# Reordering one feed-forward stage of a hybrid decoder layer: which forms are made first, and which column groups are mixed plain

## The chip, the cores and the metric

One NeuronCore of one Trainium2 chip runs the kernel. The metric is the device time of one execution in microseconds (us). The kernel before took 1992.39 us as the median of 3 runs (1990.27 to 1993.79).

## The reference, cut to what matters

One decoder layer on 256 tokens of 2048 channels, all in float32:

```
h = layer_norm(ALPHA * x + 0.5 * swiglu(x, ffn1...))
h = layer_norm(ALPHA * h + mixer(h))
h = layer_norm(ALPHA * h + 0.5 * swiglu(h, ffn2...))
swiglu(x) = (silu(x @ w_gate) * (x @ w_up)) @ w_down     # 2048 -> 5632 -> 2048
```

The change lies in the products `x @ w_gate` and `x @ w_up` of the two feed-forward networks (FFN1 and FFN2). Gate and up columns are interleaved in advance, so that a block of 512 output columns holds 256 gate and 256 matching up columns. There are 22 such blocks.

## The kernel before, in words

**Numbers.** Every float32 operand is cut in two: a high part, which ScalarE rounds off with a copy (`split`, line 149), and a low part, which VectorE gets by a subtraction (line 150). A product is three matmuls (`triple`, lines 202 to 204): high x with high w, high x with low w, low x with high w. So the first matmul of a unit needs ScalarE alone, and the second needs VectorE too. A weight unit is two k tiles of 128 rows by 512 columns; it is loaded by SyncE into `raw` or `sraw`, then split into a pair of the ring (`wring`).

**Run-ahead.** `unit` (line 188) queues the load, the split and the products of a unit. `look(3, 4)` lets three units be loaded and four be split ahead of the products. The ring has 10 pairs in the first stage of an FFN and 6 afterwards (`set_ring`, called in `second` at its unit 6), so a split waits until the products that used the pair are done. `tick` counts units whose products have been issued, and `later(n, f)` calls f after n ticks. The code's order isn't quite the order in an engine's queue: the program is put in order when it is built, and the trace shows the result.

**The gate and up stage of an FFN** (`ffn`, line 763). Blocks 0 and 1 are plain: `project` runs 8 units each, every unit giving 12 matmuls (2 k tiles, 2 halves of the tokens, 3 matmuls). When a half of a block is done, ScalarE takes silu of the gate (`sg`, line 773) and VectorE multiplies (`hb`, line 777); VectorE turns the block (`blocks`, line 664) and GpSimd writes it to DRAM.

Blocks 2 to 21 go in ten groups of two, p = 1 to 10 (`Hybrid.group`). A group computes a 2 x 2 block product (two halves of the tokens by two column blocks) over two sets of k tiles with seven products in place of eight. Products 1 to 7 use fixed linear forms of x, made once (`Seven`: the forms of k tiles 0 to 7, tiles `xs`), and sums of weight blocks, made on the way: products 5, 6 and 4 add two weight tiles on VectorE (line 390), and for product 7 a GpSimd DMA adds a weight block into an `sraw` tile in place (line 392). Each of these has two steps of 2 k tiles, 6 matmuls a step. The other k tiles are plain units: `p` for the first column block, `q` for the second.

A group is **wide** or not. A wide group takes k tiles 8 and 9 into the seven products as well: a third step of one tile (3 matmuls, weights in `eraw`, forms `xe` and `xm` made by `Extra.make`), and then only three `p` and three `q` units. A group that is not wide has four `p` and four `q` units. In matmuls: 14 x 6 + 7 x 3 + 6 x 12 = 177 in a wide group and 14 x 6 + 8 x 12 = 180 in the other. Before the change p = 1, 2, 4, 5, 7, 8 and 10 are wide, and 3, 6 and 9 are not.

The order inside a group is a string: `15p6pp72q4q3q` for a wide one, `15p6pp7p2q4q3qq` for the other, and `1p5p6p7p3q2q4qq` for the mixer's groups (`small`). After product 1 the FFN groups seed bank Y with minus X (`begin`, line 364, ScalarE), so that result (0, 0) comes out of the bank without a subtraction. The mixer's groups keep a copy of X (`n1`) and subtract it at the end (`gus` in `sum_done`, line 789, for an FFN).

**The forms.** In `first_hook`, ahead of unit 5 of block 0, six steps are planned: `sums` (the four differences), the pair for products 5 and 6, the pair for 7 and 3, the forms of 2 and 4 as they are, minus for product 1, and at last `extra.make`, at ticks 1, 3, 5, 7, 9 and 11. Block 1 ends at tick 11. `extra.make` is four subtractions of 128 x 128 (`fe`, line 312), a split of 128 x 512 (`xe`) and a negated split of 128 x 128 (`xm`, lines 323 and 324). It also holds the last use of the third raw tile of x.

**What else the groups carry.** During group 10, `get_h` and `split_h` fetch and split two tiles of h for the down product, at ticks 13 and 16 (four splits of 128 x 512). The down product (`Sliced`) follows, then LayerNorm; the mixer lies between the two FFNs.

**Buffers.** All large tiles share 41 slots (`act_tile`), PSUM banks are five `mm` and three `tr`.

Of the kernel before, what the change touches and what calls it, by code (L numbers as in the profile page):

```python
# [59 lines left out]
def layer_kernel(ctx: ExitStack, tc: tile.TileContext, a: dict, out: bass.AP):  # L60
# [6 lines left out]
    small = ctx.enter_context(tc.tile_pool(name="small", bufs=1))  # L67
# [17 lines left out]
    def mm_bank(name="mm"):  # L85
        return psum.tile([P, 512], F32, tag="mm", name=nm(name), bufs=5)
# [16 lines left out]
    def later(n, fn):  # L103
        uid[0] += 1
        heapq.heappush(todo, (step[0] + n, uid[0], fn))
# [42 lines left out]
    def split(hi, lo, src):  # L148
        S.copy(hi, src)  # L149
        V.tensor_tensor(out=lo, in0=src, in1=hi.bitcast(F32), op=ALU.subtract)  # L150
# [37 lines left out]
    def unit(load, prep, now, later_on=None):  # L188
        if load is not None:
            load()  # L190
        loaded.append((prep, now, later_on))
        advance(*ahead)

    def next_pair():
        assert len(ring) > len(prepared) + lag[0], (len(ring), len(prepared), lag[0])
        catch_up(len(ring) - 1)
        pair = ring.pop(0)
        ring.append(pair)
        return pair
# [127 lines left out]
    class Hybrid:  # L327
# [11 lines left out]
                        self.raws[n] = self.raws[n] + [t[:, i, :]]  # L339
            self.snaps = [act_tile([P, 2, 512], F32, "snap") for _ in range(2)]  # L340

        def group(self, w0, w1, done, wide=False):
            banks = {}
            small = self.small
            n2, n3, q5, n1 = [t[:, i, :] for t in self.snaps for i in range(2)]
            R = self.raws
            blocks = {"11": (w0, 0), "12": (w1, 0), "21": (w0, 2), "22": (w1, 2)}

            plan = {1: ("11", "11", None, "X"), 5: ("12", "11", ("11", "12"), "Z"), 6: ("22", "11", ("11", "22"), "X"),
                    7: (None, "12", ("12", "22"), "X"), 2: ("21", "21", None, "Y"), 4: (None, "11", ("11", "21"), "W"),  # L350
                    3: (None, "22", None, "Z")}
            after = {1: lambda: S.copy(n1, banks["X"]), 6: lambda: S.copy(n2, banks["X"]),
                     7: lambda: S.copy(n3, banks["X"]), 5: lambda: S.copy(q5, banks["Z"]),
                     2: lambda: done(0, 0, banks["Y"], n1, ALU.subtract),
                     4: lambda: done(0, 1, banks["W"], n3, ALU.subtract)}
            stops = {1, 5, 6, 7, 2, 4}

            def bank(n):
                first = n not in banks
                if first:  # L360
                    banks[n] = mm_bank()
                return banks[n], first

            def begin():
                S.mul(bank("Y")[0], banks["X"], -1.0)  # L365
            if not small:
                after[1] = begin
                after[2] = lambda: done(0, 0, banks["Y"], None, None)

            end_s = 2 if wide else 1  # L370

            def source(name, s):
                w, j0 = blocks[name]
                if s < 2:
                    return w[j0 + s]
                i = j0 // 2
                return w[4][:, i * 512:(i + 1) * 512]

            def seventh(p, s):
                load_block, src, add, b = plan[p]  # L380
                st = {}
                tiles = G if s < 2 else 1

                def load():
                    nc.sync.dma_start(R[load_block][s], source(load_block, s))

                def prep():
                    t = R[src][s]
                    if add is not None and (small or p != 7):
                        V.tensor_tensor(out=t, in0=t, in1=R[add[1]][s], op=ALU.add)  # L390
                    if not small and p == 6:
                        nc.gpsimd.dma_start(R["12"][s], source("22", s), accum_op=ALU.add)  # L392
                    pair = [v[:, :tiles * 512] for v in next_pair()]
                    split(*pair, t)
                    st["pair"] = [v.rearrange("p (g n) -> p g n", g=tiles) for v in pair]

                def now():
                    o, first = bank(b)
                    wh, wl = st["pair"]
                    for g in range(tiles):  # L400
                        if s < 2:
                            xh, xl = (v[:, 2 * s + g, :] for v in self.seven.at_[p])
                        else:
                            xh, xl = self.extra.at_[p]
                        triple(o, xh, xl, wh[:, g, :], wl[:, g, :], first and g == 0,
                               s == end_s and g == tiles - 1 and p in stops, b in "XZ" or not small)
                    if s == end_s and p in after:
                        after[p]()
                unit(load if load_block else None, prep, now)

            def plain(n, j, last=False):
                w = (w0, w1)[n]
                names = (("Y", "W"), ("Z", "X"))[n]
                st = {}

                def load():
                    st["raw"] = wpool.tile([P, 1024], F32, tag="raw", name=nm("raw"), bufs=4)
                    nc.sync.dma_start(st["raw"], w[j])

                def prep():  # L420
                    pair = next_pair()
                    split(*pair, st["raw"])
                    st["pair"] = [v.rearrange("p (g n) -> p g n", g=G) for v in pair]

                def now():
                    wh, wl = st["pair"]
                    for b in range(2):
                        o, first = bank(names[b])
                        for g in range(G):
                            k = 2 * j + g  # L430
                            triple(o, self.x.at(0, k, b), self.x.at(1, k, b), wh[:, g, :], wl[:, g, :],
                                   first and g == 0, last and g == 1, n == 1 or not small)
                    if last:
                        done(1, 0, banks["Z"], n2, ALU.add)
                        done(1, 1, banks["X"], q5, ALU.add)
                unit(load, prep, now)

            end = self.k_tiles // G - 1
            if small:
                order = "1p5p6p7p3q2q4qq"  # L440
            elif wide:
                order = "15p6pp72q4q3q"
            else:
                order = "15p6pp7p2q4q3qq"
            turn = {n: iter(range(5 if wide else 4, end + 1)) for n in range(2)}
            for i, c in enumerate(order):
                if c in "pq":
                    plain("pq".index(c), next(turn["pq".index(c)]), i == len(order) - 1)
                else:
                    for s in range(end_s + 1):  # L450
                        seventh(int(c), s)
# [311 lines left out]
    def ffn(n, x, wgu, wdn, residual, g, bt, each, first=None, between=None, nxt=None, cols=None):  # L763
# [20 lines left out]
        def sum_done(c, b, bank, snap, op):  # L784
            if snap is None:
                gu_done(c, b, bank)
                return
            t = tmp_tile([P, 512], "gus")
            V.tensor_tensor(out=t, in0=bank, in1=snap, op=op)  # L789
            half(c, b, t[:, 256:512], t[:, 0:256])  # L790
# [17 lines left out]
        seven = Seven(x.raws)  # L808
        extra = Extra(x, 2)
# [7 lines left out]
        def first_hook(j):  # L817
            if first is not None:
                first(j)
            if j == 5:  # L820
                for i, f in enumerate(seven.steps + [extra.make]):
                    later(2 * i + 1, f)
        project(wgu[0], x, KD, 512, lambda b, bank: gu_done(0, b, bank), hook=first_hook,
                between=between)
        project(wgu[1], x, KD, 512, lambda b, bank: gu_done(1, b, bank), hook=second)
# [2 lines left out]
        for p in range(1, KF // 4):  # L828
            if p == KF // 4 - 1:
                for i, q in enumerate((3, 4, 0)):  # L830
                    later(3 + 3 * i, lambda q=q: get_h(q))
                later(13, lambda: split_h(3))
                later(16, lambda: split_h(4))
            hy.group(wgu[2 * p], wgu[2 * p + 1],
                     lambda n, b, bank, snap, op, p=p: sum_done(2 * p + n, b, bank, snap, op), p % 3 != 0)
        ln = LayerNorm(0.5, residual, g, bt, each, nxt, cols, ((24, 26, 48, 50), (94, 97, 100, 103)))
        if n == 1:
            later(70, setup)
# [3 lines left out]
        order = (1, 5, 6, 7, 2, 4, 3)  # L842
# [4 lines left out]
        for p in range(2):  # L847
# [30 lines left out]
            else:  # L878
                call(len(units) - 8, widen)
            down.run(wdn[2 * p], wdn[2 * p + 1], units, forms,  # L880
                     lambda m, b, bank, sign, p=p: ln.fold(2 * p + m, b, bank, sign),
                     lambda m, b, bank, p=p: ln.evac(2 * p + m, b, bank), calls, 8 * p)
# [500 lines left out]
```

## Time and profile before

| | us |
|---|---|
| median of 3 runs | 1992.39 (1990.27 to 1993.79) |
| the profiled execution's own time | 1992.18 |
| its span in the profile | 1990.4 |
| FFN1: first product of the groups to the end of group 10 | 53.23 to 462.96 |
| FFN2: the same | 1337.24 to 1748.05 |

The span runs from the first instruction to the last; 1.8 us of the execution's time lie around it. In the profile's rows, a start is in us from the span's start, PE is TensorE, DVE is VectorE, ACT is ScalarE, POOL is GpSimd and SP is SyncE. A row of the timeline has the start, the duration, the engine and line, the operation, the tiles, the shapes and the count, and in brackets the idle time before it with what ended it.

### The profile page before, as it was taken

What the parts mean: (1) busy time and instruction counts of PE and PEld (TensorE: products, weight loads), DVE (VectorE), ACT (ScalarE), POOL (GpSimd) and SP (SyncE); (2) the same over time, 40 slices, a digit from 0 to 9 for tenths busy, and PEclk for the clock granted to TensorE, in tenths of its full rate; (3) what the DMA queues carried; (4) which work ended last, traced back from release to release, by engine and by line L of the source; (5) the groups of instructions that cost most, each with busy time, mean ns of one, the idle gap of its engine ahead of it and who ended that gap; (6) DMA issues with size and microseconds to landing.
All of it is one profiled execution on the core that took longest, in us unless ns stands there. A gap on an engine that the chain in (4) does not pass through costs nothing.

```text
span 1990.4 us, 25588 instructions
## 1 busy us (share of the span) xinstructions
PE 1965.1 (99%) x8790; PEld 1620.4 (81%) x8790; DVE 1767.2 (89%) x2153; ACT 1263.4 (63%) x1645; POOL 297.8 (15%) x517
## 2 busy tenths in 40 slices
PE   9999999999999999999999999999999999999997
PEld 7788888888888887888888888777888888888886
DVE  6999999999898889999977686779999999998886
ACT  5676766766656566666667864556666676666552
POOL 0121112112100011002223130011112211121000
PEclk9999999999999999999999999999999999999999
DMA  8888888878767666677767677658888878696763
GB/s 303 276 236 266 265 277 228 251 218 301 259 218 269 203 229 238 221 243 256 229 205 250 221 232 266 222 212 263 256 262 275 242 231 280 183 332 246 245 216 124
DMA packets 145458, 485.16 MB, mean 244 GB/s; under 512 B 20736, under 2 KB 20784, under 8 KB 145328
## 3 DMA queue, kind: packets, MB, share of 16 engines
q1 hardware_dynamic: 113328, 389.60, 57.0%
q0 software_dynamic: 32000, 93.93, 18.0%
q8 instruction: 69, 1.13, 0.2%
q14 instruction: 61, 0.50, 0.1%
HBM read 454.61 MB, written 28.84 MB: 243 GB/s over the span
## 4 chain that ended last, share of the span: by engine, by line
PE 86%; DVE 8%; issue 2%; DMA 2%; ACT 1%; SPq 0%; DVEq 0%; POOL 0%; ACTq 0%; POOLq 0%
PE mm L203 28%; PE mm L204 27%; PE mm L202 27%; DVE wring L150 4%; DVE sraw L390 2%; PE tr L202 1%; PE tr L203 1%; PE tr L204 1%; DMA sraw<-in_wgm_dram 1%; DVE blocks L664 0%; DVE hb L777 0%; ACT wring L149 0%; PE tr L629 0%; DVE gus L789 0%; DMA turn<-blocks 0%
## 5 line engine op out<-in xcount | busy, mean ns | idle before, releaser
L149 ACT CAST wring<-raw 128x1024 fp32r<-128x1024 f32 (+2 forms) x471 | 486.4, 1038 | 345.4 <-PE mm L204 236.6
L150 DVE TENSOR_TENSOR wring<-raw,wring 128x1024 fp32r<-128x1024 f32 (+2 forms) x471 | 562.1, 1202 | 108.0 <-ACT wring L149 101.1
L149 ACT CAST wring<-sraw 128x1024 fp32r<-128x1024 f32 x436 | 454.4, 1052 | 204.6 <-PE mm L204 68.8
L150 DVE TENSOR_TENSOR wring<-sraw,wring 128x1024 fp32r<-128x1024 f32 x436 | 524.0, 1218 | 20.8 <-ACT wring L149 17.5
L204 PE MATMUL mm<-wring,h 128*128 128x512 f32 (+2 forms) x1254 | 483.2, 386 | 0.9 <-DVE h L150 0.9
L203 PE MATMUL mm<-wring,h 128*128 128x512 f32 (+2 forms) x1254 | 482.5, 385 | 0.3 <-DVE wring L150 0.3
L202 PE MATMUL mm<-wring,h 128*128 128x512 f32 (+2 forms) x1254 | 482.3, 385 | 0.3 <-ACT mm L365 0.2
L203 PE MATMUL mm<-wring,xs 128*128 128x512 f32 x776 | 304.9, 393 | 4.8 <-DVE wring L150 4.7
L202 PE MATMUL mm<-wring,xs 128*128 128x512 f32 x776 | 303.6, 391 | 3.5 <-ACT wring L149 3.4
L204 PE MATMUL mm<-wring,xs 128*128 128x512 f32 x776 | 303.0, 390 | 0.0
L204 PEld LDWEIGHTS mm<-wring,h 128*128 128x128 f32 x1254 | 235.6, 188 | 48.6 <-DVE h L150 2.6
L202 PEld LDWEIGHTS mm<-wring,h 128*128 128x128 f32 x1254 | 235.6, 188 | 47.6 <-ACT h L149 1.1
L203 PEld LDWEIGHTS mm<-wring,h 128*128 128x128 f32 x1254 | 235.7, 188 | 46.7 <-DVE wring L150 0.6
L390 DVE TENSOR_TENSOR sraw<-sraw,sraw 128x1024 f32<-128x1024 f32 x168 | 203.2, 1218 | 2.2 <-DMA sraw<-in_wdq_dram 0.9
L203 PEld LDWEIGHTS mm<-wring,xs 128*128 128x128 f32 x776 | 146.0, 188 | 41.4 <-DVE wring L150 11.7
L202 PEld LDWEIGHTS mm<-wring,xs 128*128 128x128 f32 x776 | 146.0, 188 | 36.4 <-ACT wring L149 5.9
L204 PEld LDWEIGHTS mm<-wring,xs 128*128 128x128 f32 x776 | 146.2, 188 | 29.7
L203 PE MATMUL mm<-wring,x 128*128 128x512 f32 x342 | 133.5, 390 | 0.8 <-DVE wring L150 0.8
L202 PE MATMUL mm<-wring,x 128*128 128x512 f32 x342 | 132.3, 390 | 0.8 <-ACT wring L149 0.8
L204 PE MATMUL mm<-wring,x 128*128 128x512 f32 x342 | 133.1, 390 | 0.0
L666 POOL DMA_DIRECT2D hT<-blocks x176 | 97.0, 562 | 168.5 <-DVE blocks L664 115.1
L392 POOL DMA_DIRECT2D sraw<-in_gu_dram x40 | 35.7, 899 | 524.3 <-DVE sraw L390 515.8
(297 smaller groups left out, 2252.8 us busy)
## 6 DMA issues: line engine op xcount, KB each, us to landing
raw<-in_gu_dram SPq DMA_DIRECT2D x163, 512.0 KB, 4.8
sraw<-in_gu_dram SPq DMA_DIRECT2D x160, 512.0 KB, 5.3
raw<-in_dn_dram SPq DMA_DIRECT2D x140, 512.0 KB, 4.6
sraw<-in_gu_dram POOLq DMA_DIRECT2D x40, 512.0 KB, 6.0
sraw<-in_dn_dram SPq DMA_DIRECT2D x36, 512.0 KB, 6.0
hraw<-hT POOLq DMA_DIRECT2D x68, 256.0 KB, 5.1
raw<-in_w_out_dram SPq DMA_DIRECT2D x32, 512.0 KB, 4.0
eraw<-in_gu_dram SPq DMA_DIRECT2D x56, 256.0 KB, 6.1
```

The lines of the kernel that those rows point to most:

```text
L149: S.copy(hi, src)
L150: V.tensor_tensor(out=lo, in0=src, in1=hi.bitcast(F32), op=ALU.subtract)
L202: PE.matmul(o, xh, wh, start=first, stop=False, skip_group_check=again)
L203: PE.matmul(o, xh, wl, start=False, stop=False, skip_group_check=again)
L204: PE.matmul(o, xl, wh, start=False, stop=last, skip_group_check=again)
L390: V.tensor_tensor(out=t, in0=t, in1=R[add[1]][s], op=ALU.add)
L392: nc.gpsimd.dma_start(R["12"][s], source("22", s), accum_op=ALU.add)
L666: nc.gpsimd.dma_start(to.rearrange("(g r) (i f) -> i r g f", g=4, i=4)[i], t[32 * i:32 * (i + 1), :].rearrange("r (g f) -> r g f", g=4))
```

## The change

It does four things, in both FFNs:

1. `extra.make` comes first, at tick 1, and the steps of `Seven` follow at ticks 2, 4, 6, 8 and 10.
2. Group 1 is no longer wide. The groups that aren't wide are p = 1, 4 and 7; wide are 2, 3, 5, 6, 8, 9 and 10. Their numbers stay 3 and 7.
3. Group 1 has the order `1p5p6p7p2q4q3qq`.
4. Group 1 doesn't seed bank Y: it keeps a copy of X and subtracts it at the end. The other FFN groups seed as before (`seeded`), and the mixer's groups stay as they were.

```diff
-        def group(self, w0, w1, done, wide=False):
+        def group(self, w0, w1, done, wide=False, seeded=False):
...
-            if not small:
+            if seeded:
                 after[1] = begin
                 after[2] = lambda: done(0, 0, banks["Y"], None, None)
...
             elif wide:
                 order = "15p6pp72q4q3q"
+            elif seeded:
+                order = "15p6pp7p2q4q3qq"
             else:
-                order = "15p6pp7p2q4q3qq"
+                order = "1p5p6p7p2q4q3qq"
...
             if j == 5:
-                for i, f in enumerate(seven.steps + [extra.make]):
-                    later(2 * i + 1, f)
+                for i, f in enumerate([extra.make] + seven.steps):
+                    later(2 * i + 1 - (i > 0), f)
...
             hy.group(wgu[2 * p], wgu[2 * p + 1],
-                     lambda n, b, bank, snap, op, p=p: sum_done(2 * p + n, b, bank, snap, op), p % 3 != 0)
+                     lambda n, b, bank, snap, op, p=p: sum_done(2 * p + n, b, bank, snap, op),
+                     p % 3 != 1 or p == 10, p > 1)
```

Two more lines pass `seeded` in place of `not small` to the matmuls' group check.

More of the change, by code (lines that the diff above doesn't have):

```diff
@@ L405, in now @@
                         triple(o, xh, xl, wh[:, g, :], wl[:, g, :], first and g == 0,
-                               s == end_s and g == tiles - 1 and p in stops, b in "XZ" or not small)
+                               s == end_s and g == tiles - 1 and p in stops, b in "XZ" or seeded)
                     if s == end_s and p in after:
@@ L431, in now @@
                             triple(o, self.x.at(0, k, b), self.x.at(1, k, b), wh[:, g, :], wl[:, g, :],
-                                   first and g == 0, last and g == 1, n == 1 or not small)
+                                   first and g == 0, last and g == 1, n == 1 or seeded)
                     if last:
```

## The prediction

> **What bounds the kernel now.** First the page: busy shares and the chain of waits. Then TensorE's idle time by stretches, and the queues around the idle places.
>
> ```profile
> PE 1965.1 (99%) x8790; PEld 1620.4 (81%) x8790; DVE 1767.2 (89%) x2153; ACT 1263.4 (63%) x1645; POOL 297.8 (15%) x517
> PE 86%; DVE 8%; issue 2%; DMA 2%; ACT 1%; SPq 0%; DVEq 0%; POOL 0%; ACTq 0%; POOLq 0%
> ```
>
> TensorE is the bound nearly everywhere, so the change can gain only where TensorE stops. VectorE, at 89%, is the next bound, and holds 8% of the chain. The busy time by stretches, cut at FFN1's groups 1, 2, 3, 4 and 10 and at FFN2's group 1:
>
> ```profile
> 53.23:97.62 44.39, 42.01 (x178) 33.02 (x178) 43.95 (x47) 30.12 (x37) 8.60 (x13) 1.00 0.87 268
> 97.62:138.22 40.60, 40.41 (x179) 33.15 (x177) 40.10 (x46) 27.55 (x35) 6.41 (x11) 1.00 0.83 250
> 138.22:179.30 41.08, 41.08 (x181) 33.70 (x180) 39.25 (x42) 26.31 (x32) 7.71 (x12) 1.00 0.89 258
> 179.30:219.42 40.12, 40.12 (x178) 33.23 (x177) 38.07 (x43) 27.00 (x35) 7.30 (x12) 1.00 0.84 258
> ...
> 422.84:462.96 40.12, 40.12 (x178) 33.23 (x177) 40.12 (x51) 30.17 (x42) 6.08 (x11) 1.00 0.52 157
> ...
> 1337.24:1382.67 45.43, 43.30 (x177) 34.24 (x178) 44.11 (x47) 29.99 (x37) 8.51 (x13) 0.96 0.91 294
> ```
>
> The first number is the length, the fourth busy time is VectorE's. Group 4 shows the floor: 177 matmuls in 40.12 us, 0.2267 each, so a group of 180 needs 40.80. A wide group behind another wide one takes 40.60, the group behind that 41.08: 0.48 and 0.28 over the floor. Rows 2 to 4 repeat up to 422.84. Group 1 is 4.27 over its floor in FFN1 and 5.31 in FFN2, and TensorE stops ahead of it:
>
> ```profile
> 51.38 0.39 PE L204 MATMUL mm<-wring,x 128*128 128x512 f32 x1
> 53.23 0.49 PE L202 MATMUL mm<-wring,xs 128*128 128x512 f32 x1 [1.47 <-ACT wring L149]
> 54.86 0.50 PE L203 MATMUL mm<-wring,xs 128*128 128x512 f32 x1 [1.14 <-DVE wring L150]
> ...
> 1335.44 0.39 PE L204 MATMUL mm<-wring,h 128*128 128x512 f32 x1
> 1337.24 0.49 PE L202 MATMUL mm<-wring,xs 128*128 128x512 f32 x1 [1.41 <-ACT wring L149]
> 1338.93 0.50 PE L203 MATMUL mm<-wring,xs 128*128 128x512 f32 x1 [1.20 <-DVE wring L150]
> ```
>
> From start to start that is 1.85 and 1.80, so 1.62 and 1.57 lost. Lost at the groups' beginning in all: 5.89 in FFN1, 6.88 in FFN2. It isn't that VectorE had no time before:
>
> ```profile
> 39.80:49.50 9.70, 9.70 (x44) 8.04 (x43) 0.00 (x1) 0.38 (x1) 0.00 (x0) 1.00 0.96 351
> ```
>
> Its busy time there is 0.00. What stands in its queue and ScalarE's:
>
> ```profile
> 39.29 0.49 DVE L312 TENSOR_TENSOR fe<-xraw 128x128 f32<-128x128 f32 x2
> 49.50 0.42 DVE L777 TENSOR_TENSOR hb<-mm,sg 128x256 f32<-128x256 f32 x1 [9.72 <-ACT sg L773]
> 49.84 0.61 DVE L312 TENSOR_TENSOR fe<-xraw,fe 128x128 f32<-128x128 f32 x2
> 51.13 0.69 DVE L150 TENSOR_TENSOR xe<-fe,xe 128x512 fp32r<-128x512 f32 x1 [0.69 <-ACT xe L149]
> 51.74 0.28 DVE L324 SCALAR_TENSOR_TENSOR xm<-xraw,xm 128x128 fp32r<-128x128 f32 x1
> ...
> 52.99 0.71 DVE L664 STREAM_TRANSPOSE blocks<-hb 128x512 f32<-128x512 f32 x1
> 53.63 2.32 DVE L150 TENSOR_TENSOR wring<-sraw,wring 128x1024 fp32r<-128x1024 f32 x2
> ```
> ```profile
> 49.08 0.38 ACT L773 ACTIVATE sg<-mm 128x256 f32<-128x256 f32 x1 [11.47 <-PE mm L204]
> 50.48 0.62 ACT L149 CAST xe<-fe 128x512 fp32r<-128x512 f32 x1 [1.01 <-DVE fe L312]
> ...
> 51.86 0.38 ACT L773 ACTIVATE sg<-mm 128x256 f32<-128x256 f32 x1 [0.55 <-PE mm L204]
> 52.14 1.04 ACT L149 CAST wring<-sraw 128x1024 fp32r<-128x1024 f32 x1
> ```
>
> The making of tiles 8 and 9 stands among the silus and products that end block 1, and group 1's first split stands behind all of it, although both engines waited for the silu some 10 us. I read this so (argued, not shown): buffers are given out in the code's order, so `fe` waited for `sg`'s buffer and group 1's weight tiles for `xe` and `xm`, and their splits were queued last.
>
> **The change, part by part.**
>
> *Forms first.* Nothing of `extra.make` is left between block 1 and group 1. With my reading, group 1's loads and splits move ahead of the silus, into the idle 9.7 us. Six ring pairs allow five units: 1 (two steps), a plain one, 5 (two). That is five splits at 1.16 (the row of two, 2.32) and two additions (the same shape and engine; the split's 1.16 is taken): 8.1 us, which fits. Then no first matmul is late.
>
> ```profile
> sraw<-in_gu_dram SPq DMA_DIRECT2D x160, 512.0 KB, 5.3
> ```
>
> These loads then pass block 1's last ones in SyncE's queue, and the DMA share of that stretch is 0.96 already; but group 1 loads no `eraw` now, and a load lands in 5.3 us, half the idle time. If they came late, the first rival's price would hold. The steps add no wait: `extra.make` needs x's third raw tile, which is there before unit 5.
>
> *Order of group 1.* A step of two tiles gives TensorE 6 x 0.2267 = 1.36 us and VectorE 1.16, with an addition 2.32. A plain unit gives 2.72 against 1.16. Now 1, 5, plain, 6 open a wide group: product 5 wants 5.8 of VectorE (two steps and the half one) for 3.4 of TensorE. With a plain unit behind each product, VectorE's needs of 2.3, 3.5, 8.1, 9.3 us stand against 2.7, 5.4, 8.2, 10.9 at the ends of 1, plain, 5, plain. So nothing is late if the first two steps are in time. I leave 0.3 us a group for its small waits, as the 0.28 of row 3 above; the bounds are 0 and the 3.1 of the first rival. The mixer opens a group in the same kind of order without seeding:
>
> ```profile
> 745.53:772.62 27.09, 26.47 (x120) 21.22 (x119) 26.97 (x48) 18.44 (x28) 4.34 (x8) 1.00 0.63 210
> ```
>
> TensorE lost 0.6 of 27.1 us there with VectorE full.
>
> *No seeding.* ScalarE copies a bank in place of negating one, and the plain unit no longer waits for it. VectorE subtracts once more, at most 0.7 (a 128 x 512 split takes 0.69 above), in a group whose VectorE is busy 39.25 of 41.08: hidden, and 0.7 an FFN if not.
>
> *The forms' new place.* At tick 1 they meet a full VectorE: 0.49 + 0.61 + 0.69 + 0.28 = 2.07 us.
>
> ```profile
> 16.00:39.80 23.80, 23.80 (x106) 19.71 (x105) 23.19 (x27) 17.91 (x22) 0.00 (x0) 1.00 0.80 272
> 1286.00:1320.00 34.00, 33.06 (x153) 25.98 (x152) 33.92 (x54) 25.94 (x53) 3.78 (x7) 1.00 0.49 171
> ```
>
> Queued behind them are the splits of block 0's last units. But the 9.7 us of idle time after it say that the splits run far ahead of TensorE by then. In FFN2 the stretch ends at 1320, 15 us before block 1. I take 0.2 an FFN, bounds 0 and 2.07.
>
> *Which groups are wide.* The matmuls are as many. Wide now stand 2, 3; 5, 6; and 8, 9, 10 in a row. Group 10 also carries the four splits of h, and VectorE had 0.00 idle there (40.12 of 40.12) with a good start. How far its first split was ahead in group 10 (behind a group that isn't wide) and in group 2 (behind a wide one), and the place where h's splits bite:
>
> ```profile
> 413.63 1.22 DVE L150 TENSOR_TENSOR wring<-sraw,wring 128x1024 fp32r<-128x1024 f32 x1
> ...
> 91.06 1.22 DVE L150 TENSOR_TENSOR wring<-sraw,wring 128x1024 fp32r<-128x1024 f32 x1
> ...
> 430.79 1.29 DVE L150 TENSOR_TENSOR h<-hraw,h 128x512 fp32r<-128x512 f32 x2
> 431.99 1.22 DVE L150 TENSOR_TENSOR wring<-sraw,wring 128x1024 fp32r<-128x1024 f32 x1
> ...
> 433.72 0.39 PE L202 MATMUL mm<-wring,xs 128*128 128x512 f32 x1
> ```
>
> Group 10's first split ends at 414.85, 8.0 before 422.84; group 2's at 92.28, 5.3 before 97.62. The split that ends at 433.21 for the step at 433.72 has 0.5 in hand; with 2.7 less it is 2.2 late. The first matmul of a step doesn't need it (0.23), so some 1.9 is lost; counted the other way, 0.48 as behind any wide group plus two splits of h, 1.2, is 1.7. I take 1.68. Below, 0.48 if h's splits fall into waits; above, the whole debt, 2.65 plus four splits (2.58), 5.2.
>
> *The sum of an FFN's groups:* 40.80 + 0.3; three wide ones behind others that aren't, 3 x 40.12; three behind wide, 3 x 40.60; two that aren't wide, 2 x 41.08; group 10, 41.80: 407.2 us. Now: FFN1 1.62 + (462.96 - 53.23) = 411.35. FFN2's other groups go by FFN1's rows, 365.34 (409.73 - 44.39), + 45.43 + 1.57 = 412.34. The gains are 4.1 and 5.1; less 0.2 each, 8.8. From the profiled execution's own 1992.18 (span 1990.4 and 1.8 around it; 0.2 below the median of the runs) comes **1983.4 us**.
>
> **The clock gate.** A part of FFN2's loss is clock:
>
> ```profile
> 1340.00:1343.00 3.00, 3.00 (x8) 2.32 (x8) 3.00 (x5) 1.99 (x2) 1.52 (x4) 0.50 1.00 382
> ```
>
> Eight matmuls in 3 us at half the granted clock: seven of them lose some 0.2 each, 1.4 in all. It follows TensorE's two stops of 1.41 and 1.20 us; FFN1's 1.47 and 1.14 brought no such row. Without the stops the 1.4 goes too; it stands in the 5.31. [...]
>
> **The rivals.**
>
> *The queues keep their order* (the change doesn't do what it says). Group 1's splits stay behind the second silu. Then 1.62 and some 1.1 for the low half (VectorE still has `hb` and `blocks` to do, the form rows go) stay, and 0.4 at products 5 and 6: 3.1 a group in place of 0.3, so 5.6 is lost again: **1989.0**; 1990.4 if the clock halves in one FFN as now, 1991.8 in both. For it: the silu's row stands ahead whatever the forms do. Against: the forms' rows between the two silus.
>
> *VectorE's debt decides* (slower). VectorE is busy 40.10 of 40.60 in a wide group behind a wide one, so nothing is paid back in three. If the whole debt reaches TensorE, group 10 loses 5.2 in place of 1.68, and the forms 2.07 in place of 0.2, 5.4 more an FFN; and a VectorE so late in the first stage has no idle time for group 1's splits, which leaves the start as in the first rival. 1989.0 + 10.8 = **1999.8**. It decides above 1996.4, when some 7.4 of the 10.8 reach TensorE. Against: the lead at a wide group's end came back to 5.3 each time.
>
> *Group 10 hides h's splits*, with the forecast's start: 1983.4 - 2.4 = **1981.0**.
>
> **How the numbers follow.** The forecast has 0.62, the hidden splits 0.12, the kept order 0.18, VectorE's debt 0.08. A measurement tells about 0.2%, 4 us, from no change: faster is below 1988.4, slower above 1996.4. Of the kept order a fifth falls below 1988.4, so faster 0.78, within 0.2% 0.15, slower 0.07 (the debt, less a little that stays under 1996.4). The range is 1980 to 1991: the hidden splits with no small waits below (1981.0 less 0.6 and the 0.4), the kept order with the clock halved once above; the debt and odd placements are left out.
>
> **What would show it.** Right: no idle row of over 0.5 us ahead of group 1; `xe` and `xm` rows before 30 us and before 1320; the casts of group 1 ahead of block 1's last silu; half clock gone after 1335; group 1 in some 41.1 us, group 10 in some 41.8. Wrong: the casts still behind the second silu; a stop inside blocks 0 and 1; group 10 at 40.1 or above 43.

## The result, and the profile after

The changed kernel takes 1983.25 us as the median of 5 runs (1982.24 to 1984.7), the kernel before on the same chip 1992.39 (1990.27 to 1993.79). The ratio is 0.9954, with a 95% interval from 0.994 to 0.9969, so it is 0.3% to 0.6% faster. The profiled execution took 1982.51 us, with a span of 1980.7.

The page's busy shares and its chain of waits, kernel after:

```profile
PE 1960.6 (99%) x8790; PEld 1619.2 (82%) x8790; DVE 1767.2 (89%) x2155; ACT 1263.7 (64%) x1645; POOL 296.4 (15%) x517
PE 82%; DVE 11%; issue 4%; DMA 3%; ACT 1%; DVEq 0%; SPq 0%; POOL 0%; ACTq 0%; POOLq 0%
```

TensorE has the same 8790 matmuls. VectorE's share of the chain went up from 8% to 11%: some stops went, but more of the chain runs over VectorE than before. Busy time by stretches (length, then TensorE, its weight loads, VectorE, ScalarE, GpSimd, the granted clock, DMA share, GB/s), of blocks 0 and 1, of FFN1's groups 1, 3 and 10, of FFN2's group 1, and of the 3 us in it where the clock was halved before:

```profile
12.00:49.35 37.35, 37.35 (x166) 30.84 (x165) 33.53 (x41) 24.93 (x32) 1.09 (x2) 1.00 0.88 323
49.35:90.15 40.80, 40.80 (x181) 33.80 (x180) 37.36 (x39) 26.67 (x30) 6.99 (x11) 1.00 0.96 312
...
130.27:170.86 40.59, 40.41 (x178) 33.15 (x177) 40.09 (x46) 28.13 (x35) 7.04 (x11) 1.00 0.83 244
...
414.39:455.88 41.49, 40.70 (x178) 33.08 (x177) 41.49 (x53) 29.99 (x40) 7.76 (x13) 1.00 0.57 161
1329.53:1370.33 40.80, 40.80 (x181) 33.78 (x180) 36.99 (x39) 26.56 (x30) 6.75 (x11) 1.00 0.94 302
1340.00:1343.00 3.00, 3.00 (x15) 2.49 (x14) 3.00 (x4) 1.95 (x3) 0.00 (x0) 1.00 0.62 203
```

Group 1 takes 40.80 in both FFNs, which is its floor of 180 x 0.2267 to the hundredth. The last row has 15 matmuls in 3 us at full clock, where there were 8. Group 10 takes 41.49. The first row shows the new place of the forms, ticks 1 and after: TensorE busy 37.35 of 37.35, so nothing is lost there.

The queues around the old stop. First ScalarE's timeline, then VectorE's, kernel after:

```profile
40.87 1.05 ACT L149 CAST wring<-sraw 128x1024 fp32r<-128x1024 f32 x1 [2.79 <-DMA sraw<-in_gu_dram]
...
48.56 0.38 ACT L775 ACTIVATE sg<-mm 128x256 f32<-128x256 f32 x1
```
```profile
14.99 0.49 DVE L312 TENSOR_TENSOR fe<-xraw 128x128 f32<-128x128 f32 x2
...
18.68 0.68 DVE L150 TENSOR_TENSOR xe<-fe,xe 128x512 fp32r<-128x512 f32 x1
19.28 0.28 DVE L324 SCALAR_TENSOR_TENSOR xm<-xraw,xm 128x128 fp32r<-128x128 f32 x1
...
41.96 1.23 DVE L150 TENSOR_TENSOR wring<-sraw,wring 128x1024 fp32r<-128x1024 f32 x1 [2.35 <-ACT wring L149]
```

The forms are done at 19.6. Group 1's casts stand ahead of block 1's first silu now (48.56), and VectorE makes group 1's splits from 41.96 on, where it stood idle for the silu before. But stops came that the kernel before doesn't have. TensorE's timeline inside group 10 and, some 150 us later, in the down product:

```profile
426.29 0.50 PE L203 MATMUL mm<-wring,xs 128*128 128x512 f32 x1 [0.18 <-DVE wring L150]
...
430.37 0.50 PE L203 MATMUL mm<-wring,x 128*128 128x512 f32 x1 [0.61 <-DVE wring L150]
...
583.73 0.39 PE L202 MATMUL tr<-wring,xs 128*128 128x512 f32 x1
585.17 0.50 PE L203 MATMUL tr<-wring,xs 128*128 128x512 f32 x1 [1.06 <-DVE wring L150]
```

**Where the time went.** All the kernels have the same number of matmuls in each stage, so matmuls of the same number can be set against each other. They bound five stretches here: up to the 211th (in the kernel after the first of FFN1's groups, 49.35), the 1779 of the ten groups, everything up to FFN2's groups, its ten groups, and the rest up to the start of the last matmul. The times are starts and differences of starts in the profiled executions, in us; the kernels from the third row on are the experiments.

| kernel | to FFN1's groups | FFN1's groups | down, mixer, blocks 0 and 1 | FFN2's groups | rest | last matmul |
|---|---|---|---|---|---|---|
| before | 50.24 | 411.36 | 872.71 | 412.38 | 232.34 | 1979.03 |
| after | 49.35 | 406.53 | 873.65 | 406.83 | 232.97 | 1969.33 |
| `forms_first` | 49.88 | 405.47 | 872.39 | 405.41 | 232.34 | 1965.49 |
| `own_buffer` | 49.94 | 407.41 | 873.19 | 405.42 | 232.33 | 1968.29 |
| `groups_only` | 49.73 | 413.83 | 876.86 | 416.66 | 232.33 | 1989.41 |
| `spread` | 50.03 | 405.78 | 872.68 | 405.99 | 232.33 | 1966.81 |
| `h_later` | 49.22 | 405.74 | 874.55 | 405.96 | 232.34 | 1967.81 |
| `old_order` | 50.16 | 406.60 | 877.96 | 406.68 | 233.05 | 1974.45 |
| `two_plain` | 49.46 | 405.32 | 871.76 | 404.72 | 232.34 | 1963.60 |

After against before: -0.89, -4.83, +0.94, -5.55 and +0.63, in all -9.70. The groups' beginnings gained 5.2 and 6.2 (46.02 and 47.01 us for group 1 before, 40.80 after, though it has 180 matmuls now and not 177), and group 10 and the down products gave part of it back. Each row of the table is one execution. Where no edit reaches, rows differ too: after, `spread`, `h_later` and `old_order` have the same products up to the 211th matmul and take 49.22 to 50.16 us to it, and one stop of the mixer, near 793 in the kernel after, loses 0.8 to 1.7 in the nine rows. In such stretches a difference of a microsecond is not yet an effect.

### The profile page after: what moved, and what is told of

Its sections match the earlier page's. It is cut to its first block, busy times and chain, and to the rows that moved or that the text cites. A ratio compares the mean times of both kernels' runs of the same rounds, so it can differ in the third digit from the quotient of the medians.

```text
span 1980.7 us, 25615 instructions
## 1 busy us (share of the span) xinstructions
PE 1960.6 (99%) x8790; PEld 1619.2 (82%) x8790; DVE 1767.2 (89%) x2155; ACT 1263.7 (64%) x1645; POOL 296.4 (15%) x517
## 4 chain that ended last, share of the span: by engine, by line
PE 82%; DVE 11%; issue 4%; DMA 3%; ACT 1%; DVEq 0%; SPq 0%; POOL 0%; ACTq 0%; POOLq 0%
PE mm L203 26%; PE mm L204 26%; PE mm L202 26%; DVE wring L150 5%; DVE sraw L390 1%; DMA hraw<-hT 1%; DMA raw<-in_dn_dram 1%; DMA sraw<-in_wgm_dram 1%; PE tr L203 1%; PE tr L204 1%; PE tr L202 1%; DVE sraw L579 0%; ACT wring L149 0%; DVE blocks L666 0%; DVE gus L791 0%
```

## The experiments

`forms_first`, `own_buffer`, `groups_only` and `spread` ran on one chip, beside a kernel before of 1993.34 us; `h_later`, `old_order` and `two_plain` on one chip, beside a kernel before of 1992.15 us.

**The forms' order alone.** The kernel before, with part 1 of the change and nothing else:

```diff
-                for i, f in enumerate(seven.steps + [extra.make]):
-                    later(2 * i + 1, f)
+                for i, f in enumerate([extra.make] + seven.steps):
+                    later(2 * i + 1 - (i > 0), f)
```

> The kernel before with the forms of tiles 8 and 9 made first (ticks 1, 2, 4, 6, 8, 10) and nothing else: group 1 stays wide, seeded and in the order 15p6pp72q4q3q. Theory (the queue order did it: group 1's splits stood behind block 1's silus because the forms' buffers did): the stops ahead of group 1 (1.62 and 1.57 us) and the half clock go, group 1 takes 40.3 to 41.3 us in both FFNs because product 5 still wants 5.8 us of VectorE for 3.4 of TensorE, group 10 stays at 40.1: 1981 us, between 1979.5 and 1983. Rival (the plain order of group 1 did it): the stops stay or half of group 1's 4.3 and 5.3 us stays, 1987 to 1991.

It took 1978.47 us (1977.86 to 1980.16), ratio 0.9929, interval 0.9914 to 0.9944: faster than the kernel before, and by its ratio than the kernel after too, though that one ran beside another kernel before and the two intervals just touch (0.9944 and 0.9940). It is also less than the 1979.5 to 1983 that were expected. The windows of FFN1's groups 1 and 10 and of FFN2's group 1, kernel `forms_first`:

```profile
49.88:90.00 40.12, 40.12 (x179) 33.22 (x178) 37.89 (x42) 27.22 (x34) 6.39 (x11) 1.00 0.97 319
...
415.24:455.35 40.11, 40.11 (x178) 33.22 (x177) 40.11 (x51) 29.25 (x40) 6.63 (x12) 1.00 0.53 152
1327.74:1367.86 40.12, 40.12 (x178) 33.22 (x177) 37.67 (x42) 26.89 (x34) 6.15 (x10) 1.00 0.91 286
```

Group 1 stands at the floor of a wide group, 177 x 0.2267 = 40.12, and not at the 40.3 to 41.3 that were expected, though it is wide, opens with 1, 5, plain, 6 and seeds its bank. So the order of the forms is the whole gain, and the other three parts of the change together cost 3.84 us at the last matmul of the two profiles (1969.33 against 1965.49): 1.06 and 1.42 in the groups, 1.26 and 0.63 in the down products and what follows, less 0.53 at the start.

**The other parts alone.** The changed kernel with the forms made last again:

```diff
-                for i, f in enumerate([extra.make] + seven.steps):
-                    later(2 * i + 1 - (i > 0), f)
+                for i, f in enumerate(seven.steps + [extra.make]):
+                    later(2 * i + 1, f)
```

> The changed kernel with the forms made last again, as before: group 1 is plain in the new order and unseeded, and the other groups are wide as in the changed kernel. Theory: the casts of group 1 stand behind block 1's second silu, TensorE stops for 1.6 us ahead of group 1 and for some 1.1 on its first low half: 1989 us, between 1987 and 1991. Rival (the plain order did it): 1983 us, no stop ahead of group 1.

It took 1999.19 us (1997.61 to 2002.6), ratio 1.0034, interval 1.0021 to 1.0047: slower than before, and outside what either theory gave. Group 1 of both FFNs and the 4 us behind its first stops in FFN1, kernel `groups_only`, then TensorE's timeline there, ScalarE's, and SyncE's queue (start, time from the first issue to the last, tiles, count):

```profile
49.73:97.81 48.08, 43.40 (x181) 34.64 (x180) 43.31 (x45) 29.97 (x35) 8.06 (x12) 0.96 0.92 306
1340.42:1391.11 50.69, 44.77 (x182) 35.74 (x180) 43.59 (x45) 29.98 (x35) 7.88 (x12) 0.93 0.90 300
56.00:60.00 4.00, 4.00 (x13) 3.17 (x12) 4.00 (x4) 1.14 (x2) 2.37 (x4) 0.61 1.00 390
```
```profile
53.60 0.50 PE L202 MATMUL mm<-wring,xs 128*128 128x512 f32 x1 [2.35 <-ACT wring L149]
...
55.49 0.66 PE L203 MATMUL mm<-wring,xs 128*128 128x512 f32 x1 [1.15 <-DVE wring L150]
```
```profile
51.57 1.04 ACT L149 CAST wring<-raw 128x1024 fp32r<-128x1024 f32 x1
52.50 1.99 ACT L149 CAST wring<-sraw 128x1024 fp32r<-128x1024 f32 x2
```
```profile
34.84 10.95 SPq L418 DMA_DIRECT2D raw<-in_gu_dram  x5
45.85 5.07 SPq L385 DMA_DIRECT2D sraw<-in_gu_dram  x8
```

Group 1 is 7.3 and 9.9 us over its floor of 40.80. Five loads of plain units stand first in SyncE's queue, held up for 10.95 us, and the eight loads that the first products need stand behind them, from 45.85 on. At the opening it isn't these loads that ScalarE waits for, though: a plain unit's cast (from `raw`) comes behind the second silu, and product 1's casts follow it without a pause, at 52.50. Casts that wait for a load come only later, at 65.87 and 68.32, for 2.3 us in all. With the forms first, the kernel after issues a plain load at 34.23 and the first four of the others from 34.61 on, so the order of the forms decides the order of that queue too.

```profile
34.23 0.33 SPq L418 DMA_DIRECT2D raw<-in_gu_dram  x1
34.61 2.46 SPq L385 DMA_DIRECT2D sraw<-in_gu_dram  x4
```

**A buffer of its own.** The prediction argued that `fe` waited for `sg`'s small buffer. The kernel before, with `fe` in the large slots:

```diff
-            f = tmp_tile([P, 2, 2, P], "fe")
+            f = act_tile([P, 2, 2, P], F32, "fe")
```

> The kernel before with one line changed: the four differences of tiles 8 and 9 (fe) get one of the 41 large slots in place of one of the six small ones that silu's result also takes. The forms are still made last. Theory (buffers are given out in the code's order, so fe waited for the silu's buffer and group 1's loads for the forms'): fe, xe and xm run before the silu, group 1's casts too, and the time is that of the kernel with the forms first, 1981 us, between 1979.5 and 1984. Rival (the forms' place in the code is what counts, they end block 1 anyway): 1990 to 1993.

It took 1981.7 us (1981.44 to 1982.67), ratio 0.9945, interval 0.993 to 0.9959: within the theory's range, though `forms_first` took 3.2 us less. ScalarE's timeline and SyncE's queue, kernel `own_buffer`, and the queue of the kernel before:

```profile
40.05 0.62 ACT L149 CAST xe<-fe 128x512 fp32r<-128x512 f32 x1 [2.22 <-DVE fe L312]
...
46.35 1.05 ACT L149 CAST wring<-sraw 128x1024 fp32r<-128x1024 f32 x1 [5.47 <-DMA sraw<-in_gu_dram]
...
49.13 0.38 ACT L773 ACTIVATE sg<-mm 128x256 f32<-128x256 f32 x1
```
```profile
35.04 4.39 SPq L418 DMA_DIRECT2D raw<-in_gu_dram  x4
39.49 0.90 SPq L385 DMA_DIRECT2D sraw<-in_gu_dram  x2
```
```profile
35.39 4.33 SPq L418 DMA_DIRECT2D raw<-in_gu_dram  x4
39.77 0.90 SPq L385 DMA_DIRECT2D sraw<-in_gu_dram  x2
```

With the forms as late in the plan as before, `xe` and `xm` and group 1's first casts now come ahead of the silu. So it was the shared buffer that tied the forms to the silu. One half of the prediction's reading falls, though: the loads were not held for `xe` and `xm`. Both kernels issue the first of them at nearly the same time, 39.5 and 39.8; in the kernel before only the splits stood behind. What `own_buffer` doesn't reach is that time: it waits 5.47 us for the load, and its FFN1 group 1 takes 42.12, while `forms_first` casts the first one at 42.11. In FFN2 both stand at 40.12.

**Other groups plain.** The changed kernel with groups 1, 5 and 9 plain in place of 1, 4 and 7, so that wide ones stand in threes and group 10 stands behind a plain one:

```diff
-                     p % 3 != 1 or p == 10, p > 1)
+                     p % 4 != 1, p > 1)
```

> The changed kernel with other groups that aren't wide: 1, 5 and 9 in place of 1, 4 and 7, so three wide ones stand in a row twice (2 to 4, 6 to 8), and group 10 stands behind one that isn't wide. Theory (group 10 costs because it starts 2.7 us shorter and carries h's splits; a third wide group without them costs the same 0.48 as a second): groups 3, 4, 7 and 8 at 40.60, 5 and 9 at 41.05, group 10 at 40.12, in an FFN 1.0 to 1.3 us less than the changed kernel's groups; 1981 us, or 1979 if the down product's stops go too. Rival (VectorE's debt grows in a row of three): groups 4 and 8 at 41.5 or more, 1983 us or above.

It took 1980.51 us (1978.3 to 1980.88), ratio 0.9935, interval 0.9918 to 0.9952. FFN1's groups 3, 4 and 10, kernel `spread`:

```profile
130.95:171.57 40.62, 40.44 (x178) 33.14 (x177) 40.16 (x46) 27.59 (x35) 7.03 (x11) 1.00 0.82 248
171.57:212.18 40.61, 40.42 (x178) 33.15 (x177) 40.11 (x46) 28.13 (x35) 8.11 (x13) 1.00 0.84 263
...
415.69:455.81 40.12, 40.12 (x179) 33.23 (x177) 40.12 (x51) 29.27 (x40) 6.62 (x12) 1.00 0.52 153
```

The third wide group in a row costs what the second does, so VectorE doesn't fall further behind from group to group. An FFN's groups take 0.75 and 0.84 us less than in the kernel after, where the theory had 1.0 to 1.3. Group 10 behind a plain group is at its floor, splits of h and all, and TensorE doesn't stop at 585. The 1.37 us of group 10 and the stops in the down products come from the place of the plain groups.

**The splits of h later.** In the changed kernel's group 10:

```diff
-                later(13, lambda: split_h(3))
-                later(16, lambda: split_h(4))
+                later(18, lambda: split_h(3))
+                later(22, lambda: split_h(4))
```

> The changed kernel, with the third and fourth split of h in group 10 moved from ticks 13 and 16 to ticks 18 and 22. Theory A (the stops of 0.88 and 0.45 us in group 10 come from h's two splits standing in VectorE's queue just ahead of the splits that a wide group's early products need): group 10 falls from 41.49 to 40.6 us in both FFNs, as any wide group behind a wide one, so 1.8 us less in all, near 1981.5; if the down product's stops of 1.33 and 0.62 us are the same lateness handed on, they go too and the time is near 1979.5. Theory B (VectorE as a whole is late behind two wide groups, whatever the place of h's splits): group 10 stays at 41.5 or the same loss turns up later in the group or in the down product, 1983 +- 1.

It took 1980.98 us (1978.9 to 1985.67), ratio 0.9944, interval 0.993 to 0.9957. Group 10 of FFN1 (FFN2's takes 40.60 as well) and the stop in the down product, kernel `h_later`:

```profile
414.37:454.96 40.59, 40.41 (x178) 33.15 (x177) 40.55 (x51) 29.28 (x39) 7.77 (x13) 1.00 0.57 158
```
```profile
585.08 0.50 PE L203 MATMUL tr<-wring,xs 128*128 128x512 f32 x1 [1.82 <-DVE wring L150]
```

Theory A holds for group 10: of its 1.37 us, 0.9 were the splits of h standing ahead of a weight split, and 0.48 is what any wide group behind a wide one loses. It doesn't hold for the down product: FFN1's stop there grew (from start to start 2.28 us, so 2.05 lost, against 1.22 after), while FFN2's of 0.51 went. So FFN1's stop isn't just group 10's lateness handed on.

**The old opening of group 1.** The changed kernel with group 1 seeded and opening as before:

```diff
-                     p % 3 != 1 or p == 10, p > 1)
+                     p % 3 != 1 or p == 10, p > 0)
```

> The changed kernel with group 1 of each FFN given back its old opening (1, 5, plain, 6, plain, plain) and its seeded bank, still not wide and with the forms made first. Theory A (the order of the forms alone removes the stop, since group 1's splits are all made in VectorE's 9.7 idle us): group 1 stays within 0.3 us of 40.80 and the time is that of the changed kernel, 1983 +- 1. Theory B (the prediction's reason: without a plain unit behind each product VectorE's need of 5.8 us stands against 3.4 us of TensorE, so product 5 or 6 is late): group 1 takes 42 to 43 us, 1.5 to 2.4 us more an FFN, 1986 to 1988.

It took 1986.01 us (1984.14 to 1988.24), ratio 0.9968, interval 0.9956 to 0.998. Group 1 of both FFNs, the 3 us behind the down product's stop, and that stop, kernel `old_order`:

```profile
50.16:90.95 40.79, 40.79 (x181) 33.79 (x180) 36.11 (x37) 26.25 (x30) 6.21 (x11) 1.00 0.96 311
1334.72:1375.52 40.80, 40.80 (x182) 33.78 (x180) 36.60 (x38) 26.57 (x31) 6.94 (x12) 1.00 0.94 299
589.00:592.00 3.00, 3.00 (x8) 2.32 (x7) 3.00 (x5) 1.02 (x1) 0.00 (x0) 0.50 0.78 272
```
```profile
587.51 0.49 PE L203 MATMUL tr<-wring,xs 128*128 128x512 f32 x1 [1.81 <-DVE wring L150]
```

Theory A is right on group 1, which is at its floor with the old order and the seeded bank: neither the new order nor the missing seed was needed. Its time is missed. The 1986.01 us lie in theory B's range, but not for theory B's reason: the kernel loses 3.6 us from 585 to 593 where the kernel after loses 1.22 (2.09 in the stop, then some 0.2 on each of eight matmuls at half clock), and 1.24 more in one stop of the mixer at 966. Why an edit of group 1 moves a stop 500 us later stays open.

**A second plain unit ahead of product 6**, in the kernel `forms_first`:

```diff
-                order = "15p6pp72q4q3q"
+                order = "15pp6p72q4q3q"
...
-                order = "15p6pp7p2q4q3qq"
+                order = "15pp6p7p2q4q3qq"
```

> The kernel before with the forms made first (1978.47 us), and in every group a second plain unit moved ahead of product 6 (opening 1, 5, plain, plain, 6, plain). It asks whether the 0.48 us that a wide group loses behind a wide one, and the 0.28 of the group behind that, is lateness at the opening alone. Theory A (the opening: two products of half units in a row want more of VectorE than TensorE's time there): wide groups behind wide ones fall from 40.60 to 40.12 and the groups behind them from 41.08 to 40.80; three of each in an FFN, 4.6 us less in all, near 1974. Theory B (VectorE is full over the whole group, 40.10 of 40.60 us, and is the bound there): the loss moves to a later product, the pair still takes 81.68 us, 1978.5 +- 1.

It took 1977.66 us (1977.19 to 1979.83), ratio 0.9927, interval 0.9915 to 0.9939. FFN1's groups 2 and 3, then FFN2's group 2, kernel `two_plain`:

```profile
89.58:130.81 41.23, 40.73 (x179) 33.07 (x178) 40.71 (x46) 28.12 (x35) 7.05 (x11) 1.00 0.85 249
130.81:171.60 40.79, 40.79 (x181) 33.78 (x180) 39.23 (x41) 26.84 (x31) 7.30 (x12) 1.00 0.87 258
...
1366.66:1407.28 40.62, 40.42 (x179) 33.16 (x178) 40.10 (x46) 28.20 (x35) 7.03 (x11) 1.00 0.85 251
```

Each theory holds for one group. The plain group behind a wide one drops from 41.08 to 40.80, its floor, six times out of six: its 0.28 was the opening. The wide group behind a wide one keeps its 0.48, or more (41.23 once): there VectorE is busy 40.10 of 40.62, and the loss only moves to another product. In the profiles that is 1.89 us less than `forms_first` at the last matmul; by the runs, the two can't be told apart.

## Why the prediction was right, and where it was not

The forecast was 1983.4, the measured median 1983.25. The profiled execution, from which the forecast was counted, took 1982.51, so 9.7 us were gained where the sum had 8.8. So close a hit is partly luck: several terms were off by about a microsecond and cancelled.

- **Forms first.** Right in what it does, and shown to be the whole gain by `forms_first`. All the signs came: no stop ahead of group 1, `xe` and `xm` before 30 us and before 1320, group 1's casts ahead of block 1's last silu, no half clock after 1335, and groups 1 and 10 at 40.80 and 41.49 for some 41.1 and 41.8. The reading of the cause was half right: `own_buffer` shows that `fe` waited for the silu's small buffer, and that group 1's loads did not wait for `xe` and `xm`. Nor do group 1's loads pass block 1's last ones, as the step said: in the kernel before and in the kernel after, SyncE issues block 1's loads (line 229) ahead of them, the last by 33.5 and 32.3 us. What the loads for products pass is plain loads of their own group, four of which went first in the kernel before and one in the kernel after.
- **Order of group 1 and no seeding.** The step said that without a plain unit behind each product, product 5 would want 5.8 us of VectorE for 3.4 of TensorE. It counted VectorE's needs from the first product on. But the first splits are made before that product starts, so the lead covers the shortage: `old_order` has group 1 at 40.80, `forms_first` at 40.12. The 0.3 us a group that this step left for small waits were 0, 0.6 in all, and the added subtraction was hidden, as the step said.
- **The forms' new place.** 0.2 us an FFN were taken; in FFN1 the row from 12.00 to 49.35 shows 0.
- **Which groups are wide.** Three wide behind wide ones at 40.60, plain ones behind wide at 41.03 to 41.05: as forecast. (One more, FFN2's group 9, took 40.88.) Group 10 lost 1.37, not 1.68. The mechanism, 0.48 and splits of h, was right by `h_later`; the splits cost 0.9 and not 1.2. An FFN's groups took 406.53 and 406.83 where the step had 407.2, 1.0 less in all.
- **What was not in the sum.** The prediction ended the effect of part 2 at the end of group 10. The down product of FFN1 lost 1.22, that of FFN2 0.51. The four kernels with groups 8, 9 and 10 wide in a row lost 1.2 to 3.6 between 585 and 600; the others, `spread` with its other threes among them, don't stop there. What differs before it is in the waits of VectorE for ScalarE's casts between 470 and 600 us (time in all, times, longest), here of after, `h_later` and `forms_first`, one fence each:

```profile
DVE wring L150 <- ACT wring L149: 6.2, 7, 1.7
DVE h L150 <- ACT h L149: 3.1, 2, 2.5
```
```profile
DVE wring L150 <- ACT wring L149: 9.1, 7, 3.2
```
```profile
DVE h L150 <- ACT h L149: 5.5, 3, 2.7
DVE wring L150 <- ACT wring L149: 2.9, 7, 0.7
```

The waits for casts of weights are 6.2 us or more in the four kernels that stop and 4.0 or less in the five that don't. With the waits for casts of h, though, the sums are 9.3, 9.1 and 8.4 us here, so the idle time in all doesn't give the length of the stop. From 560 to 590 VectorE is busy 30.00 of 30.00 us in all three kernels, so what was idle before can't be made up by 585; that is how I read it, but it isn't shown: no run took that idle time away by itself. What makes the casts later there was not settled. Against this loss stood 0.89 us less ahead of FFN1's groups, nearly all of it in the first 12 us, where the start differs by a microsecond from kernel to kernel.

- **The rivals.** The queues that keep their order did not come. `groups_only`, where the forms are last again and the casts of group 1 stand behind the second silu, is near to that rival, though not the same, since the forms' rows stand between the silus there. It lost 7.3 and 9.9 us a group, not 3.1, with a plain unit's cast ahead of product 1's and with the clock halved. The price took the start of before and left out that the change also reorders the queues of plain and mixed units. VectorE's debt doesn't grow over three wide groups (`spread`). The hidden splits of h did not come either.

## What to carry to other kernels

When an engine idles next to a full queue, look for what ties the head of that queue, here one small buffer shared with an operation that comes late; one reordered list then brought more than the whole change. Undo the parts of a change one at a time even when it helps: the other three parts here together cost 3.8 us of what the first one gained. And where an engine is busy 99% of a stage, an edit's price may fall due more than 100 us later, so the sum must run to the next stretch in which that engine idles.

## What the runs showed of the hardware that was not expected

The granted clock halved behind stops of 1.15 to 2.41 us, and not always behind stops of the same length. Between FFN1's groups and the last matmul the traces show it six times: once in the kernel before, four times in `groups_only`, once in `old_order`. In the kernel before it lasted 3.41 us:

```profile
1339.67:1343.08 3.41, 3.41 (x9) 2.65 (x9) 3.41 (x5) 1.99 (x2) 1.93 (x5) 0.50 0.99 380
```

In it matmuls start 0.43 us apart (1340.62, 1341.05), behind it 0.23 (1343.38, 1343.61), so each of eight lost 0.2. The mean clock of the windows around the other five comes to some 3.4 us too: in `groups_only`, 0.82 from 1344 to 1347 and 0.61 from 1347 to 1350 make 3.42 at half clock. It came after two stops of 1.41 and 1.20 us (FFN2 of the kernel before), after 2.35 and 1.15 (both FFNs of `groups_only`), after one of 2.41 (FFN2 of `groups_only`, 1362.15), after the 1.81 of `old_order`, and in the down product of `groups_only`, where TensorE idles 1.85 of the 5 us from 590 to 595 and the clock is 0.62 from 594 to 598. It did not come after 1.47 and 1.14 (FFN1 of the kernel before, 1.00 throughout group 1) nor after the 1.82 of `h_later`, which stands on the same line of the down product as the 1.81 of `old_order`. Here are the 20 us around these two stops, of `h_later` and then of `old_order`:

```profile
580.00:590.00 10.00, 8.18 (x37) 6.35 (x36) 10.00 (x12) 5.36 (x6) 0.68 (x2) 1.00 0.67 213
590.00:600.00 10.00, 10.00 (x46) 8.29 (x45) 9.96 (x26) 9.56 (x13) 0.39 (x1) 1.00 0.92 304
```
```profile
580.00:590.00 10.00, 8.19 (x33) 6.00 (x32) 10.00 (x12) 3.90 (x4) 0.00 (x0) 0.95 0.51 157
590.00:600.00 10.00, 10.00 (x41) 8.17 (x40) 10.00 (x24) 7.69 (x9) 1.07 (x2) 0.88 0.88 289
```

TensorE idles 1.82 and 1.81 us in the first 10 of them; in `h_later` the clock stays at 1.00, in `old_order` it is 0.95 and 0.88. So the length of the stop doesn't tell these two apart, and what does was not shown: no run moved one of these stops by itself. Where the half clock came, it cost some 1.6 us on top of the stop, eight matmuls at 0.2.
